# The two feed-forward products of a trunk layer by seven block products in place of eight

## The chip, the cores and the metric

The kernel runs on one core of a Trainium2 chip. The metric is the device time of one execution in microseconds (us), as a median of runs. The core has five engines that work side by side from lists of instructions of their own: TensorE (PE) for matrix products, VectorE (DVE), ScalarE (ACT), GpSimd (POOL), and SyncE (SP), which here issues nearly all transfers between DRAM and the on-chip memory. Within one list the order is fixed; between lists semaphores keep it.

## What is computed

One layer on 1024 positions of width 1024, all in float32. Three branches (an mLSTM, a differential attention, a retention) are merged and projected; then the feed-forward follows, the part that matters here:

```python
x = x + rmsnorm(y @ w_out, g[1])
h2 = rmsnorm(x, g[2])
a, u = jnp.split(h2 @ w_ffn_in, 2, axis=-1)       # [1024, 1024] @ [1024, 2 x 2816]
f = (jax.nn.silu(a) * u) @ w_ffn_out              # [1024, 2816] @ [2816, 1024]
x = x + rmsnorm(f, g[3])
```

## The kernel before

TensorE multiplies parts of 12 bits: every float32 operand is split into a high part (a cast on ScalarE, L96) and a low part (a subtraction on VectorE, L97), and `mm3` (L101 to L103) issues three matrix products of 128x128 by 128x512 for each pair of tiles. Accumulators are banks of PSUM of 128x512, four of kind "d" and four of kind "m".

All dense products of the kernel form one stream of blocks (`stream`), whose weights are loaded two blocks ahead into `ws` (two tiles), and split one block ahead into `wh` and `wl` (four tiles each). A pool "T" has 33 tiles of 4 KB for each partition and holds whatever is kept long; blocks that are marked `own` have their weights there. A pool "s2k" has eleven tiles of 128x512.

The last stage before the feed-forward is `out_blocks`. Its last quarter, `run_last`, makes the second half of the sequence tile by tile; `norm_steps` (L876 to L884) then turn each tile of the product `z` into x2 and the normalized h2, with a load of x, a square on ScalarE (L220), three single-column steps (L214, L215 on GpSimd) and wide operations on VectorE (L879, L880, L884). `transposed` (L235 to L238) turns four tiles of h2 at a time on TensorE, and splits them into `h2T`.

The hidden width of 2816 is 22 blocks of 128. For each of them `proj_half` multiplies the block's 128 columns of gate weights and of up weights (stationary, from wh/wl) with h2T (moving, 512 positions): 8 contraction tiles, 2 halves of the sequence, 3 passes each. `gated` applies Silu on ScalarE (L964), `hidden` multiplies on VectorE (L959) and splits the result into `ah`, `al`, which stay on the chip. `up_first` runs block 0 with the first half of the sequence while the second half is still being normalized. Down runs by groups of hidden blocks (2, then five times 4): for each of 8 tiles of the sequence and 2 halves of the columns it accumulates the group in PSUM and adds that into `f` (L992, L994). The last group, `last_down`, has its own weights in the big pool, and takes each finished tile through the last norm (L1016 to L1024, squares at L1037) while the next is multiplied.

SyncE issues loads and stores in the order of its list, each of them waiting for the one eight places before it.

## Time and profile before

| | us |
|---|---|
| median of three runs | 2748.53 |
| lowest and highest run | 2746.95, 2749.08 |
| span of the profiled execution | 2744.7 |
| TensorE busy in the span | 2711.7 |
| VectorE busy | 1217.4 |
| ScalarE busy | 964.1 |
| GpSimd busy | 99.2 |

The profile is of one execution on the chip. Its span runs from the first to the last recorded instruction; the time of a run holds a little more than that. An engine is busy while it executes an instruction; the matrix products of TensorE overlap, so their sum of durations is more than their busy time, and their pace is read from the distances of their starts. The chain of waits follows the work that ended last backwards. The feed-forward takes the span from about 1992 us to the end.

### The profile page before, as it was taken

To read this page: it belongs to the slowest core of one execution; us is meant where nothing else is said; L and a number is where in the kernel's file an instruction comes from. 1 tells how busy PE (TensorE), PEld (TensorE's weight loads), DVE (VectorE), ACT (ScalarE), POOL (GpSimd) and SP (SyncE) were. 2 spreads that over 40 slices of the span, in tenths; PEclk is the share of its full clock that TensorE was granted. 3 is DMA by queue.
4 is the path that set the end of the run, shared out by engine and by line. 5 is a ranking of instruction groups with operands and counts; after the bars stand their busy time and mean duration, and the time that the engine had idled before them with its cause. 6 is when DMAs were issued, how large, how long until landed. Compare 5 with 4: busy or idle time off the path is not lost.

```text
span 2744.7 us, 34888 instructions
## 1 busy us (share of the span) xinstructions
PE 2711.7 (99%) x14049; PEld 2280.3 (83%) x14049; DVE 1217.4 (44%) x2679; ACT 964.1 (35%) x1901; POOL 99.2 (4%) x165
## 2 busy tenths in 40 slices
PE   7999999999999999999999999999999999999998
PEld 6888989888888888888989888888888888888886
DVE  5565564544554545543333354354642223232315
ACT  5644443334444444444333354232521111111112
POOL 0000000000000000000000000000100000000000
PEclk9999999999999999999999999999999999999999
DMA  4121112322222213211111155422521111111113
GB/s 143 50 59 54 58 59 58 92 77 67 74 77 62 77 51 85 58 43 51 47 54 47 54 161 167 145 88 82 191 65 47 39 54 39 54 44 55 47 40 138
DMA packets 225052, 202.67 MB, mean 74 GB/s; under 512 B 9373, under 2 KB 181870, under 8 KB 224890
## 3 DMA queue, kind: packets, MB, share of 16 engines
q1 hardware_dynamic: 223456, 198.25, 23.7%
q10 hardware_dynamic: 1434, 2.20, 0.3%
q8 instruction: 110, 1.80, 0.3%
q14 instruction: 52, 0.43, 0.0%
HBM read 158.44 MB, written 33.59 MB: 70 GB/s over the span
## 4 chain that ended last, share of the span: by engine, by line
PE 94%; DVE 3%; ACT 2%; DMA 1%; issue 1%; POOL 0%; ACTq 0%; SPq 0%; POOLq 0%; DVEq 0%
PE ps L101 28%; PE ps L102 28%; PE ps L103 28%; PE ps L630 2%; PE ps L667 2%; PE ps L656 1%; PE ps L460 1%; PE ps L468 1%; DVE wl L97 0%; PE ps L428 0%; ACT wh L96 0%; PE ps L235 0%; DMA s2k<-branch 0%; PE ps L685 0%; DVE f L994 0%
## 5 line engine op out<-in xcount | busy, mean ns | idle before, releaser
L101 PE MATMUL ps<-hh,wh 128*128 128x512 f32 x1408 | 571.0, 406 | 1.6 <-DVE hl L238 1.6
L103 PE MATMUL ps<-hh,wl 128*128 128x512 f32 x1408 | 556.5, 395 | 0.0
L102 PE MATMUL ps<-hl,wh 128*128 128x512 f32 x1408 | 556.5, 395 | 0.0
L96 ACT CAST wh<-ws 128x1024 fp32r<-128x1024 f32 x219 | 228.7, 1047 | 730.0 <-PE ps L102 472.6
L97 DVE TENSOR_TENSOR wl<-ws,wh 128x1024 fp32r<-128x1024 f32 (+1 forms) x219 | 266.3, 1219 | 449.8 <-ACT wh L96 433.7
L103 PEld LDWEIGHTS ps<-hh,wl 128*128 128x128 f32 x1408 | 264.3, 188 | 63.3
L101 PEld LDWEIGHTS ps<-hh,wh 128*128 128x128 f32 x1408 | 265.1, 188 | 55.5 <-DVE hl L238 1.9
L102 PEld LDWEIGHTS ps<-hl,wh 128*128 128x128 f32 x1408 | 264.9, 188 | 53.7
L102 PE MATMUL ps<-h2l,wh 128*128 128x512 f32 x704 | 278.3, 395 | 0.0
L101 PE MATMUL ps<-h2h,wh 128*128 128x512 f32 x704 | 277.9, 395 | 0.3 <-ACT h2h L237 0.3
L103 PE MATMUL ps<-h2h,wl 128*128 128x512 f32 x704 | 278.0, 395 | 0.0
L101 PE MATMUL ps<-wh,hh 128*128 128x256 f32 (+1 forms) x768 | 219.8, 286 | 0.0
L102 PE MATMUL ps<-wl,hh 128*128 128x256 f32 (+1 forms) x768 | 216.1, 281 | 0.0
L103 PE MATMUL ps<-wh,hl 128*128 128x256 f32 (+1 forms) x768 | 215.8, 281 | 0.0
L101 PEld LDWEIGHTS ps<-h2h,wh 128*128 128x128 f32 x704 | 131.9, 187 | 32.7 <-ACT h2h L237 0.6
L102 PEld LDWEIGHTS ps<-h2l,wh 128*128 128x128 f32 x704 | 132.0, 187 | 32.2
L103 PEld LDWEIGHTS ps<-h2h,wl 128*128 128x128 f32 x704 | 132.0, 187 | 32.2
L101 PE MATMUL ps<-bh,wh 128*128 128x512 f32 x384 | 153.0, 398 | 1.0 <-ACT bh L96 1.0
L102 PE MATMUL ps<-bl,wh 128*128 128x512 f32 x384 | 151.8, 395 | 0.2 <-DVE bl L97 0.2
L103 PE MATMUL ps<-bh,wl 128*128 128x512 f32 x384 | 151.5, 395 | 0.0
L101 PEld LDWEIGHTS ps<-wh,hh 128*128 128x128 f32 x768 | 144.8, 189 | 0.2
L102 PEld LDWEIGHTS ps<-wl,hh 128*128 128x128 f32 x768 | 144.8, 189 | 0.2
(215 smaller groups left out, 4160.9 us busy)
## 6 DMA issues: line engine op xcount, KB each, us to landing
ws<-in_w_in_dram SPq DMA_DIRECT2D x110, 512.0 KB, 4.0
ws<-in_w_ffn_in_dram SPq DMA_DIRECT2D x44, 512.0 KB, 4.0
gate<-s2k SPq DMA_DIRECT2D x48, 256.0 KB, 2.0
gl<-gate SPq DMA_DIRECT2D x24, 512.0 KB, 6.2
s2k<-branch SPq DMA_DIRECT2D x48, 256.0 KB, 5.6
ws<-in_w_ffn_out_dram SPq DMA_DIRECT2D x22, 512.0 KB, 4.3
dk<-dk SPq DMA_DIRECT2D x64, 128.0 KB, 2.3
ws<-in_w_out_dram SPq DMA_DIRECT2D x16, 512.0 KB, 3.9
```

The costliest lines, as they stand in the source:

```text
L96: nc.scalar.copy(hi, src)
L97: nc.vector.tensor_sub(lo, src, hi.bitcast(F32))
L101: nc.tensor.matmul(ps, lh, rh, start=start, stop=False)
L102: nc.tensor.matmul(ps, lh, rl, start=False, stop=False)
L103: nc.tensor.matmul(ps, ll, rh, start=False, stop=stop)
L460: nc.tensor.matmul(ps[:, :P], k_t[c // 4][:, j, half_cols(c)], q_t[c // 4][:, j, half_cols(c)], start=j == 0, stop=j == 1)
L468: nc.tensor.transpose(ps[:, j * P:(j + 1) * P], hn[:, j * P:(j + 1) * P], ident)
L630: nc.tensor.matmul(ps[:, :b - a], d["q", qb // 4][:, c, half_cols(qb)], d["k", n][i][:, c, :b - a], start=i == 0, stop=i == 1)
L656: nc.tensor.transpose(ps[:, i * P:(i + 1) * P], u["sb"][0][:, kb * P:(kb + 1) * P], ident)
L667: nc.tensor.matmul(o_ps[:, :P], u["at"][kb // 4][:, half_cols(kb)], v[kb // 4][:, kb % 4, vc], start=kb == 0, stop=kb == qb)
```

## The change

Up and down are each written as a product of 2 x 2 blocks, and each by Strassen's method in Winograd's form: seven block products of sums of blocks in place of eight block products. For up, the left operand h2 is cut by halves of the sequence and halves of the contraction (A11 to A22), the right by halves of the contraction and by gate and up columns (B11 to B22), one hidden block at a time. For down, it is halves of the sequence by even and odd hidden blocks on the left, even and odd hidden blocks by halves of the columns on the right.

`turned` takes the place of `transposed`: it keeps the unsplit transposed tile too (`hx`), and `left_sums` makes the sums S1 to S4 of it and splits them. `Up.sums` makes the sums of the weights (T1 to T4) on VectorE. The seven products of a block share two banks of PSUM: a bank is read after a product and further products are then added into it. Blocks 0 and 1 run interleaved; from block 2 on the order is p1, p2, p6, p5, p7, p3, p4. The hidden values are not split; `keep_hidden` stores for each pair of blocks three of them and four sums, which GpSimd makes, into tables `hid` in DRAM: seven tiles of 256 KB a pair. All of up is done before down. `down` runs seven products after another; each goes through all 11 pairs, and for each pair it reads one tile of `hid`, splits it, makes the weights' sum in place, splits that (both into wh/wl), and multiplies four tiles of the sequence: 12 matrix products. All row blocks of `w_ffn_out` are loaded once and stay.

The core of the diff, with blank lines left out; `Block`, `stream` and the other stages are as before:

```diff
-    h2T = Act("h2")
-        turns = {sh: transposed(h2T, z[sh], sh, 80) for sh in range(2)}
+        turns = {sh: turned(z[sh], sh, 80) for sh in range(2)}
...
         def run_last(w):
             before = []
+            ups[0].load()
...
             z[0][:] = [None] * 4
+            ups[0].split("B1")
...
-    def hidden(blk, sh, pu):
...
-    def gated(blk, sh, pa):
...
-    def up_first(blk, turns):
...
-    def down(blks, st, ch, w, first):
...
-    def last_down(blks):
...
+    NP = FB // 2
+    ROLES = ("A11", "A12", "A22", "S1", "S2", "S3", "S4")
+    hid = {r: dram.tile([NP, P, HALF], F32, name=f"hid_{r}") for r in ROLES}
...
+    def turned(src, sh, g):
+        for kt in range(KT) if sh == 0 else (4, 5, 0, 1, 6, 7, 2, 3):
+            ps = psum()
+            for i in range(4):
+                nc.tensor.transpose(ps[:, i * P:(i + 1) * P], src[i][:, kt * P:(kt + 1) * P], ident)
+            col = pcol[:, g + kt:g + kt + 1]
+            role, q = "A" + str(sh + 1) + str(kt // 4 + 1), kt % 4
+            if (role, q // 2) not in h2x:
+                h2x[role, q // 2] = big([P, 2, HALF], name="hx")
+            x = h2x[role, q // 2][:, q % 2, :]
+            if role == "A21":
+                nc.scalar.activation(x, ps, AF.Copy, scale=col)
+            else:
+                h, l = h2.slot(role, q)
+                nc.scalar.activation(h, ps, AF.Copy, scale=col)
+                nc.vector.tensor_scalar(x, ps, col, None, op0=ALU.mult)
+                nc.vector.tensor_sub(l, x, h.bitcast(F32))
+            yield
+    def left_sums():
+        for i in range(2):
+            nc.vector.tensor_add(h2x["A22", i], h2x["A21", i], h2x["A22", i])
+            h2.put("S1", i, h2x["A22", i])
+        yield
+        for i in range(2):
+            nc.vector.tensor_sub(h2x["A22", i], h2x["A22", i], h2x["A11", i])
+            h2.put("S2", i, h2x["A22", i])
...
+    class Up:
+        def __init__(self, blk, own=False):
+            self.blk, self.own, self.w = blk, own, {}
+        def load(self):
+            self.raw = [pool.tile([P, KT, P], F32, tag="ws", bufs=N_WS, name=nm("ws")) if not self.own else big([P, KT, P], name="ws")
+                        for _ in range(2)]
+            for u in range(2):
+                nc.sync.dma_start(self.raw[u], cols_of(w_ffn_in, u * FF + self.blk * P)[0])
+        def sums(self):
+            a, u = self.raw
+            self.t13 = big([P, KT, P], name="t13")
+            self.t24 = big([P, KT, P], name="t24")
+            lo, hi = slice(0, 4), slice(4, 8)
+            nc.vector.tensor_sub(self.t13[:, lo, :], u[:, lo, :], a[:, lo, :])
+            nc.vector.tensor_sub(self.t13[:, hi, :], u[:, hi, :], u[:, lo, :])
+            nc.vector.tensor_add(self.t24[:, lo, :], self.t13[:, hi, :], a[:, lo, :])
+            nc.vector.tensor_sub(self.t24[:, hi, :], a[:, hi, :], self.t24[:, lo, :])
...
+        def product(self, ps, right, left, more):
+            wh, wl = self.w.pop(right)
+            for q in range(4):
+                mm3(ps, (wh[:, q, :], wl[:, q, :]), h2.slot(left, q), q == 0 and not more, q == 3, more)
+        def p1(self):
+            self.x = psum(True)
+            self.product(self.x, "B11", "A11", False)
+            self.a = half_tile()
+            nc.scalar.copy(self.a, self.x)
+        def p2(self):
+            z = psum(True)
+            self.product(z, "B21", "A12", False)
+            nc.vector.tensor_add(self.a, z, self.a)
+            nc.scalar.activation(self.a, self.a, AF.Silu)
...
+        def p7(self):
+            self.product(self.x, "T3", "S3", True)
+            nc.vector.tensor_add(self.e, self.x, self.e)
+        def p3(self):
+            self.product(self.y, "B22", "S4", True)
+            nc.vector.tensor_add(self.b, self.y, self.b)
+            nc.vector.tensor_mul(self.b, self.a, self.b)
+            self.h = [self.b, self.e]
+        def p4(self):
+            self.product(self.x, "T4", "A22", True)
+            s = half_tile()
+            nc.scalar.activation(s, self.x, AF.Silu)
+            nc.vector.tensor_mul(self.e, s, self.e)
+            self.x = self.y = self.a = self.b = self.e = None
+    def keep(role, p, t):
+        nc.sync.dma_start(hid[role][p], t)
+    def keep_hidden(first, second):
+        p = first.blk // 2
+        (a11, a21), (a12, a22) = first.h, second.h
+        keep("A11", p, a11)
+        keep("A12", p, a12)
+        keep("A22", p, a22)
+        s = [half_tile() for _ in range(4)]
+        nc.gpsimd.tensor_tensor(s[0], a21, a22, op=ALU.add)
+        keep("S1", p, s[0])
+        nc.gpsimd.tensor_tensor(s[2], a11, a21, op=ALU.subtract)
+        keep("S3", p, s[2])
+        nc.gpsimd.tensor_tensor(s[1], s[0], a11, op=ALU.subtract)
+        keep("S2", p, s[1])
+        nc.gpsimd.tensor_tensor(s[3], a12, s[1], op=ALU.subtract)
+        keep("S4", p, s[3])
+        first.h = second.h = None
+    def feed_forward(ups, turns):
+        a, b = ups[:2]
+        a.sums()
+        for what in ("T24", "T13", "B2"):
+            a.split(what)
+        a.p1()
+        a.p2()
+        b.load()
+        b.sums()
+        b.split("B1")
+        b.p1()
+        for _ in turns:
+            pass
+        z[1][:] = [None] * 4
+        sums = left_sums()
+        next(sums)
+        b.p2()
+        for what in ("T24", "T13", "B2"):
+            b.split(what)
+        a.p5(False)
+        next(sums)
+        b.p5(False)
+        a.p6()
+        next(sums)
+        b.p6()
+        a.p7()
+        next(sums)
+        b.p7()
...
+        keep_hidden(a, b)
+        for n, u in enumerate(ups[2:], 2):
+            after = ups[n + 1] if n + 1 < len(ups) else None
+            u.p1()
+            if after is not None:
+                after.load()
+            u.p2()
+            u.p6()
+            if after is not None:
+                after.sums()
+            u.p5()
+            if after is not None:
+                after.split("B1")
+            u.p7()
+            if after is not None:
+                after.split("T24")
+            u.p3()
+            if after is not None:
+                after.split("T13")
+            u.p4()
+            if after is not None:
+                after.split("B2")
+            if n % 2:
+                keep_hidden(ups[n - 1], u)
+        for r in ROLES:
+            h2.drop(r)
+    def down():
+        gains[3] = gain(3)
+        f = [None] * NT
+        w = []
+        def load(p):
+            w.append([big([P, D], name="wd") for _ in range(2)])
+            for i in range(2):
+                nc.sync.dma_start(w[p][i], w_ffn_out[(2 * p + i) * P:(2 * p + i + 1) * P, :])
+        def right(role, p):
+            b11, b12, b21, b22 = (w[p][i][:, halfs(ch)] for i in range(2) for ch in range(2))
+            if role == "B11":
+                return b11
+            if role == "T1":
+                nc.vector.tensor_sub(b12, b12, b11)
+                return b12
...
+            nc.vector.tensor_sub(b12, b21, b12)
+            return b12
+        def operands(role_l, role_r, p):
+            t = half_tile()
+            nc.sync.dma_start(t, hid[role_l][p])
+            h = pool.tile([P, 2, HALF], F32R, tag="wh", bufs=N_WH, name=nm("wh"))
+            l = pool.tile([P, 2, HALF], F32R, tag="wl", bufs=N_WL, name=nm("wl"))
+            split_sbuf(h[:, 0, :], l[:, 0, :], t)
+            split_sbuf(h[:, 1, :], l[:, 1, :], right(role_r, p))
+            return h, l
+        def step(ps, o, j, first, last, more):
+            h, l = o
+            c = slice(j * P, (j + 1) * P)
+            mm3(ps, (h[:, 0, c], l[:, 0, c]), (h[:, 1, :], l[:, 1, :]), first and not more, last, more)
+        def product(role_l, role_r, ps, more):
+            for p in range(NP):
+                if role_r == "B11":
+                    load(p)
+                o = operands(role_l, role_r, p)
+                for j in range(4):
+                    step(ps[j], o, j, p == 0, p == NP - 1, more)
...
+        f[:] = [big([P, D], name="f") for _ in range(NT)]
+        px = [psum(True) for _ in range(4)]
+        product("A11", "B11", px, False)
+        for j in range(4):
+            nc.scalar.copy(f[j][:, halfs(0)], px[j])
+        py = [psum() for _ in range(4)]
+        product("S1", "T1", py, False)
...
+        product("S4", "B22", py, True)
+        for j in range(4):
+            nc.vector.tensor_add(f[j][:, halfs(1)], py[j], f[j][:, halfs(1)])
+        product("S3", "T3", px, True)
...
+        pz = [psum() for _ in range(4)]
+        product("A12", "B21", pz, False)
+        for j in range(4):
+            nc.vector.tensor_add(f[j][:, halfs(0)], pz[j], f[j][:, halfs(0)])
+        s2 = [small([P, 2], "s2", bufs=8) for _ in range(NT)]
+        held = []
+        for p in range(NP):
+            o = operands("A22", "T4", p)
+            if p < NP - 4:
+                for j in range(4):
+                    step(px[j], o, j, False, False, True)
+                if p < 4:
+                    xt = x2_of(p)
+                    for ch in range(2):
+                        squares(p, ch, s2[p])
+                    finish(p, xt, s2[p])
+                    f[p] = None
+                    squares(p + 4, 1, s2[p + 4])
+            else:
+                held.append(o)
+        xts = [x2_of(j + 4) for j in range(4)]
+        for j in range(4):
+            for n, o in enumerate(held):
+                step(px[j], o, j, False, n == 3, True)
+            st = j + 4
+            squares(st, 0, s2[st], px[j])
+            nc.vector.tensor_copy(f[st][:, halfs(0)], px[j])
+            finish(st, xts[j], s2[st])
...
-    groups = [[0, 1]] + [list(range(i, i + 4)) for i in range(2, FB, 4)]
...
-            blocks += [up_first(blk, turns)] if blk == 0 else up_blocks(blk)
...
+    ups = [Up(i, own=i == 1) for i in range(FB)]
...
     for _ in dense:
         pass
+    feed_forward(ups, turns)
+    down()
```

Three places where the lists of the engines differ. Names are those of the program with a number; "waits" lists the semaphores that a row waits for (DMAHW: a transfer's).

SyncE, where the second half of the sequence is normalized (`xr` is x, `x2_dram` takes x2, `ws` are weights). Before:

```order
L876 DMA xr_3778_18307<-in_x_dram 128x1024 [waits DMAHW1_49,DMAHW0_49]
L876 DMA xr_3792_18369<-in_x_dram 128x1024
L139 DMA ws_3862_18756<-in_w_ffn_out_dram 128x2x512 [waits DMAHW6_49,DMAHW2_49,DVE_49]
L881 DMA x2_dram_78<-xr_3778_18307 128x1024 [waits DMAHW3_49,DVE_49]
L881 DMA x2_dram_78<-xr_3792_18369 128x1024 [waits DVE_49]
```

After:

```order
L876 DMA xr_3775_18310<-in_x_dram 128x1024 [waits DMAHW3_49,Activation_49]
L881 DMA x2_dram_78<-xr_3775_18310 128x1024 [waits DMAHW6_49,DVE_49]
L876 DMA xr_3790_18375<-in_x_dram 128x1024 [waits DMAHW7_49,PE_49]
L876 DMA xr_3805_18440<-in_x_dram 128x1024 [waits DMAHW0_49,PE_49]
L876 DMA xr_3815_18486<-in_x_dram 128x1024 [waits DMAHW1_49,PE_49]
L881 DMA x2_dram_78<-xr_3790_18375 128x1024 [waits DMAHW2_49,DVE_49]
```

Before, the x of the first and of the second tile were asked for one after the other, ahead of the first store of x2; now the store of the first tile's x2 stands between them.

VectorE, same place. Before, the last two tiles' norms and what follows them (L959 is block 0, L238 the transposed tiles; `xs`, `xv` are single columns):

```order
L879 SCALAR_TENSOR_TENSOR z_3767_18253<-z_3767_18253,xr_3819_18482,gain1_3661_17745 128x1024 [waits Pool_49]
L880 TENSOR_TENSOR xr_3816_18477<-xr_3816_18477,z_3767_18253 128x1024 [waits DMAHW6_49,DVE_49]
L214 TENSOR_SCALAR xv_3824_18493<-xs_3822_18490 128x1 [waits Activation_49]
L884 TENSOR_SCALAR z_3767_18253<-xr_3816_18477,xr_3823_18492 128x1024 [waits Pool_49]
L959 TENSOR_TENSOR s2k_3829_18528<-ps_3830_18530,s2k_3829_18528 128x512 [waits PE_49,Activation_49]
L97 TENSOR_TENSOR al_3832_18556<-s2k_3829_18528,ah_3831_18555 128x512 [waits Activation_49]
L238 SCALAR_TENSOR_TENSOR h2l_3835_18566<-ps_3833_18560,pcol_83,h2h_3834_18565 128x512 [waits Activation_49]
L238 SCALAR_TENSOR_TENSOR h2l_3835_18566<-ps_3836_18569,pcol_83,h2h_3834_18565 128x512 [waits Activation_49]
```

After, from the second tile's sum of x and z on (t13, t24 are weight sums, L97 with `wl` a split of weights):

```order
L880 TENSOR_TENSOR xr_3790_18375<-xr_3790_18375,z_3764_18255 128x1024 [waits DMAHW7_49]
L1043 TENSOR_TENSOR t13_3826_18510<-ws_3768_18262,ws_3767_18261 128x512 [waits DMAHW4_49,PE_49]
L1044 TENSOR_TENSOR t13_3826_18510<-ws_3768_18262 128x512
L215 TENSOR_SCALAR xv_3803_18415<-xs_3801_18412 128x1 [waits Activation_49]
L1045 TENSOR_TENSOR t24_3827_18511<-t13_3826_18510,ws_3767_18261 128x512 [waits DVE_49,PE_49]
L884 TENSOR_SCALAR z_3764_18255<-xr_3790_18375,xr_3802_18414 128x1024 [waits Pool_49]
L1046 TENSOR_TENSOR t24_3827_18511<-ws_3767_18261,t24_3827_18511 128x512 [waits DVE_49]
L215 TENSOR_SCALAR xv_3809_18446<-xs_3807_18443 128x1 [waits Activation_49]
L879 SCALAR_TENSOR_TENSOR z_3765_18257<-z_3765_18257,xr_3808_18445,gain1_3661_17752 128x1024 [waits Pool_49]
L97 TENSOR_TENSOR wl_3829_18517<-t24_3827_18511,wh_3828_18516 128x1024 [waits Activation_49]
L880 TENSOR_TENSOR xr_3805_18440<-xr_3805_18440,z_3765_18257 128x1024 [waits DMAHW0_49,DVE_49]
```

Before, the norms stood nearly alone; now weight sums and splits of blocks 0 and 1 stand between the steps of the norms.

SyncE at the end of up. Before, the weights of the last blocks and of the last group of down:

```order
L139 DMA ws_4263_22192<-in_w_ffn_in_dram 128x8x128 [waits DMAHW5_49,DVE_49]
L139 DMA ws_4270_22252<-in_w_ffn_in_dram 128x8x128 [waits DMAHW6_49,DVE_49]
L139 DMA ws_4277_22316<-in_w_ffn_out_dram 128x2x512 [waits PE_49]
L139 DMA ws_4278_22318<-in_w_ffn_out_dram 128x2x512 [waits PE_49]
L139 DMA ws_4279_22320<-in_w_ffn_out_dram 128x2x512 [waits PE_49]
```

After, the last stores of hidden values and sums, and the first reads of down:

```order
L1109 DMA hid_A22_88<-s2k_4310_21506 128x512 [waits DMAHW0_49,DVE_49]
L1109 DMA hid_S1_89<-s2k_4312_21553 128x512 [waits DMAHW1_49,Pool_49]
L1109 DMA hid_S3_91<-s2k_4314_21555 128x512 [waits DMAHW2_49,Pool_49]
L1109 DMA hid_S2_90<-s2k_4313_21554 128x512 [waits DMAHW3_49,Pool_49]
L1109 DMA hid_S4_92<-s2k_4315_21556 128x512 [waits DMAHW4_49,Pool_49]
L1229 DMA s2k_4331_21583<-hid_A11_86 128x512 [waits DMAHW5_49,Activation_49]
L1229 DMA s2k_4336_21607<-hid_A11_86 128x512 [waits DMAHW6_49,Activation_49]
```

The reads of `hid_A11` come in the list behind the stores of the last pair, which wait for GpSimd; before, only weights were moved there.

## Rows read from the trace of the kernel before

**Rows 1.** The page: busy time by engine; the chain of waits by engine.
```profile
PE 2711.7 (99%) x14049; PEld 2280.3 (83%) x14049; DVE 1217.4 (44%) x2679; ACT 964.1 (35%) x1901; POOL 99.2 (4%) x165
...
PE 94%; DVE 3%; ACT 2%; DMA 1%; issue 1%; POOL 0%; ACTq 0%; SPq 0%; POOLq 0%; DVEq 0%
```

**Rows 2.** Windows in the feed-forward: length, busy by engine, granted clock, DMA share, GB/s.
```profile
2064.00:2155.00 91.00, 91.00 (x392) 73.10 (x391) 21.11 (x25) 18.04 (x25) 0.00 (x0) 1.00 0.15 47
2155.00:2694.00 539.00, 539.00 (x2313) 433.38 (x2311) 145.65 (x179) 86.66 (x112) 0.00 (x0) 1.00 0.16 50
```

**Rows 3.** Groups by line, up (page: busy, mean ns, idle) and down (durations).
```profile
L101 PE MATMUL ps<-h2h,wh 128*128 128x512 f32 x704 | 277.9, 395 | 0.3 <-ACT h2h L237 0.3
...
L101 PE MATMUL ps<-wh,ah x352: 389/395/397, 2041.0 to 2733.4; 128*128 128x512 f32 x176
```

**Rows 4.** Timeline of TensorE: start, duration, instruction; up, then the last group of down.
```profile
2012.07 0.40 PE L103 MATMUL ps<-h2h,wl 128*128 128x512 f32 x1
...
2016.27 0.40 PE L101 MATMUL ps<-h2h,wh 128*128 128x512 f32 x1
...
2727.32 0.39 PE L101 MATMUL ps<-wh,ah 128*128 128x512 f32 x1
...
2733.66 0.39 PE L102 MATMUL ps<-wl,ah 128*128 128x512 f32 x1
2733.89 0.39 PE L103 MATMUL ps<-wh,al 128*128 128x512 f32 x1
```

**Rows 5.** Groups of VectorE and ScalarE from 1940 on: busy, mean ns, idle before.
```profile
L97 DVE TENSOR_TENSOR wl<-ws,wh 128x1024 fp32r<-128x1024 f32 x71 | 86.5, 1223 | 217.4 <-ACT wh L96 205.4 <-PE ps L102 11.8
...
L97 DVE TENSOR_TENSOR al<-s2k,ah 128x512 fp32r<-128x512 f32 x44 | 30.3, 688 | 15.8 <-ACT ah L96 15.8
L1022 DVE SCALAR_TENSOR_TENSOR f<-f,xr,gain 128x512 f32<-128x512 f32 x16 | 11.3, 748 | 5.8 <-POOL xr L215 5.8
...
L879 DVE SCALAR_TENSOR_TENSOR z<-z,xr,gain 128x1024 f32<-128x1024 f32 x8 | 10.2, 1282 | 3.3 <-POOL xr L215 3.3
...
L884 DVE TENSOR_SCALAR z<-xr,xr 128x1024 f32<-128x1024 f32 x8 | 6.0, 753 | 2.7 <-POOL xr L215 2.6
...
L96 ACT CAST wh<-ws 128x1024 fp32r<-128x1024 f32 x69 | 72.5, 1051 | 368.9 <-PE ps L102 176.1 <-PE ps L103 103.6 <-issue 78.6
L96 ACT CAST ah<-s2k 128x512 fp32r<-128x512 f32 x44 | 27.2, 618 | 111.6 <-DVE s2k L959 111.6
L964 ACT ACTIVATE s2k<-ps 128x512 f32<-128x512 f32 x44 | 26.2, 595 | 99.7 <-PE ps L103 99.6
```

**Rows 6.** Groups of GpSimd, whole span: busy, mean ns, idle before.
```profile
L215 POOL TENSOR_TENSOR dfac<-dv,expo 128x1 f32<-128x1 f32 x64 | 35.2, 550 | 661.0 <-DVE dv L214 661.0
L215 POOL TENSOR_TENSOR xr<-xv,expo 128x1 f32<-128x1 f32 x32 | 25.5, 801 | 1044.3 <-DVE xv L214 1044.3
```

**Rows 7.** Timeline of TensorE: last product of out, first of up, first transposes of the second half.
```profile
1991.85 0.40 PE L103 MATMUL ps<-wh,yl 128*128 128x512 f32 x1
1992.09 0.39 PE L101 MATMUL ps<-h2h,wh 128*128 128x512 f32 x1
...
2003.28 0.93 PE L235 MATMUL ps<-ident,z 128*128 128x128 f32 x7
```

**Rows 8.** DMA issues, whole span: count, KB each, median us from issue to landing.
```profile
ws<-in_w_ffn_in_dram SPq DMA_DIRECT2D x44, 512.0 KB, 4.0
gate<-s2k SPq DMA_DIRECT2D x48, 256.0 KB, 2.0
...
xr<-in_x_dram SPq DMA_DIRECT2D x8, 512.0 KB, 5.5
...
x<-x_dram SPq DMA_DIRECT2D x8, 512.0 KB, 9.2
```

**Rows 9.** Windows at the end of the span, columns as in rows 2.
```profile
2694.00:2700.00 6.00, 6.00 (x28) 4.99 (x27) 2.36 (x6) 1.45 (x4) 0.55 (x1) 1.00 1.02 414
...
2734.00:2739.00 5.00, 0.28 (x2) 0.00 (x0) 3.45 (x8) 1.45 (x4) 0.52 (x1) 1.00 0.28 105
...
2740.00:2744.00 4.00, 0.00 (x0) 0.00 (x0) 1.68 (x3) 0.00 (x0) 0.00 (x0) 0.50 0.35 131
```

165 lines of the change are left out of this document (87 added, 78 removed).

## The prediction

> **What bounds the kernel now.** I read the busy shares and the chain of waits first: TensorE is busy for 2711.7 of 2744.7 us and carries 94% of the chain [rows 1]. The windows over the feed-forward say the same more sharply: from 2064 to 2155 (up) and from 2155 to 2694 (up and down by turns) TensorE has no idle time at all, VectorE is busy for 146 and ScalarE for 87 of 539 us, and the DMA engines run at a share of 0.16 [rows 2]. So a matrix product that goes away is worth its whole interval there, until something else becomes late. The interval is read from starts in the timeline, not from the durations (0.39 to 0.40 us, which overlap): 18 intervals from 2012.07 to 2016.27 give 0.2333 us, and 28 from 2727.32 to 2733.66 give 0.2265 us [rows 4]. The slower rate stands where one operand lies in the small pool wh/wl, the faster in the last group, whose weights lie in the big one.
>
> **What goes.** Up has 704 products of each of three passes, down 352 [rows 3]: 2112 + 1056 = 3168. Afterwards up has 22 blocks x 7 x 4 x 3 = 1848, down 7 x 11 x 4 x 3 = 924: 2772. TensorE's list of instructions is shorter by 397 rows, so the change does what it says. Before: 2976 x 0.2333 + 192 x 0.2265 = 737.8 us. After, all operands of down in wh/wl: 2772 x 0.2333 = 646.7. **Gain 91.1 us.** The unknown is the rate of down's new products: both operands now come from wh/wl, which no row shows. At 0.2265 it is 6.2 us more gain, as much the other way at 0.240 (the same step upward); I take 0.2333, the rate with one operand there.
>
> **Steady up stage.** A block is 7 x 12 x 0.2333 = 19.6 us of TensorE. VectorE has in it 4 sums and one split of 512, 3 splits of 1024, 5 evacuations of 512: 10 x 0.69 + 3 x 1.22 = 10.6 us; ScalarE 3 x 1.05 + 0.62 + 5 x 0.60 = 6.8 us [rows 5]. Both fit. GpSimd gets four sums of 128x512 for each pair of blocks; its only rows are 128x1 at 0.55 to 0.80 us [rows 6]. I price the wide one as that start-up plus VectorE's 0.69 for the same width, 1.24 us; the bounds are 0.69 (no dearer than VectorE) and 1.93 (0.55 + two times 0.69). At 5 us in 39 us nobody waits for it. The Trainium skill, GPSIMD Engine Reference, 3.1 Elementwise, has a sum of 2048 elements at 4497 ns on GpSimd and 2293 on VectorE; by that ratio, an estimate, the wide sum takes 1.35 us, and the time below grows by 0.4. Seven stores of 256 KB and four weight loads of 512 KB per pair are 3.8 MB in 39.2 us, some 97 GB/s, against 414 GB/s where the trace is saturated [rows 9]. The tightest chain is the second weight half of the next block: its buffer is free 1.5 us into the block, it lands after 4.0 us [rows 8], two sums, the evacuations behind them in VectorE's order and a copy follow, and product seven at 11.2 us needs that; I find 2.1 us of slack. Cost 0, bounds 0 and 0.5 us x 20 = 10 us.
>
> **Front (start of the feed-forward).** Before, TensorE ended `out` at 1992.1 and had 48 products of block 0 to run until the transposes of the second half at 2003.28 [rows 7]: the norms were covered. Now A22, A21 and the sums S1 and S2 must exist before the two first blocks go beyond p1 and p2, and VectorE makes most of it in order. In its order, the sum of x and z of the second tile of that half (first row of the second VectorE piece, L880) waits for an x load that is now issued behind the store of the tile before it; with 5.5 us to land [rows 8] I put it at 1990.5. From there to the split of S2 there are 18 operations of 1024 at 1.22, two at 1.28, three at 0.75 and 20 of 512 at 0.69 [rows 5], and five tiny ones: 22.0 + 2.6 + 2.3 + 13.8 + 0.7 = 41.4 us. That ends at 2032 with no waits; with 4 us of waits for ScalarE's casts and squares between (bounds 0 and 4, and 0.04 to 0.07 us less per operation where such are back to back), between 2029 and 2036. From there 90 products remain of both blocks, 21.0 us: 2050 to 2057. With TensorE never waiting, the 168 products and 32 transposes (0.93 us for seven [rows 7], so 4.3 us) from 1991.5 would end at 2035.0. **Stall 15 to 22 us, taken 18**; bounds 10 (a third of VectorE's work slipped under waits that I count) and 24.
>
> **Junction from up to down.** On SP's list the first read of `hid_A11` stands behind the store of the last `hid_S4`, and that one waits for GpSimd, though A11 was stored long before. From the end of the last product: Silu 0.60, multiply 0.69, four sums on GpSimd 4 x 1.24 = 5.0, semaphores and issue 0.6 (an estimate, no row has them apart), landing 2.5 (between 2.0 for 256 KB and 4.0 for 512 KB [rows 8], nearer the first), cast 0.62, split 0.69 [rows 5]: **10.7 us** in which TensorE has nothing. With GpSimd at 0.69 or 1.93 it is 8.5 or 13.5, with a landing of 5.5 us 13.7; with both late 17. The sums of GpSimd run beside VectorE's sums for T1 and its splits. The Trainium skill, SBUF — State Buffer, Who interferes with whom, says that a VectorE instruction with two inputs in SBUF and a GpSimd instruction that reads SBUF exclude each other; that speaks against this part, and by it each of the four could wait one 0.69 us operation more, 2.8 us in all, and the time would be 2696 in place of the 2693 below. No row here shows the two together, so the sum goes without it; the bounds hold it.
>
> **The clock.** The granted clock is 1.00 to 2739, 5 us after the last product, and 0.50 from 2740 on [rows 9]: 2.4 GHz falls to 1.2 after that much idleness. A gap of 10.7 us is longer, so down starts at half speed. No row shows how it comes back; I take one step of 12 products at 5.6 instead of 2.8 us, **2.8 us**, bounds 0 and 5.6. The same happens in the front, but there TensorE runs behind VectorE anyway.
>
> **Steady down, and its end.** A step is 12 products, 2.8 us; it needs two casts of 512 (1.24 us of ScalarE) and two splits and one sum (2.07 us of VectorE), and a read of 256 KB, 94 GB/s. Reads run ahead by the 11 buffers of s2k, splits by 4 of wh/wl, and the two sets of PSUM banks change places, so evacuations are hidden: cost 0. In the last product VectorE has 11 x 2.07 + four finishes of two L1022 and two adds, 4 x 2.9 [rows 5], + 4 x 0.69 = 37.1 us against 30.8 of TensorE; a lead of some 3 to 6 us covers part: **3.6 us**, bounds 0 and 8. After the last product 10.4 us came before (it ends at 2733.89 + 0.39 [rows 4]); the same chain of square, norm, scale, add and store remains: +0.3, bounds -1 and +4.
>
> **Sum.** 2744.7 - 91.1 + 18 + 10.7 + 2.8 + 3.6 + 0.3 = 2689.0 us of span. The three runs have a median of 2748.5, 3.8 above the span: 2693. All lows together (10, 8.5, 0, 0, -1, rate -6.2) give 2669; all highs (24, 17, 5.6, 8, 4, blocks 10, rate 6.2) 2732.
>
> **Rivals.** *Only the products count.* Front and junction are hidden, as the front is before [rows 7]: 2744.7 - 91.1 + 3.8 = 2657. For it: TensorE bound everywhere in [rows 2]. Against it: nothing stands in TensorE's list to fill the junction, and VectorE's work in the front is longer than the products beside it. 6%.
> *Down runs one step after another.* If cast, sum and splits do not run ahead, a step takes 2 x 0.62 + 3 x 0.69 = 3.3 us instead of 2.8 [rows 5], 77 x 0.5 = 39 us: 2732. For it: every operand of every product is now loaded and split anew, where before a split weight tile served eight row tiles. Against it: four buffers, and both engines have time over. 10%.
> *Slower: each up block waits for its weights.* The second half of the next block's weights is asked for only when a split frees its buffer, and SP's list puts it among stores that wait for GpSimd. With the landing at 9.2 us, which loads of 512 KB took in the last stretch [rows 8], instead of 4.0, the slack of 2.1 is overrun by 3.1 us, x 20 blocks = 62 us: 2755, slower than before. It decides from a landing of 8.9 us (55 us / 20 = 2.8 over the slack). Against it: 9.2 us belong to a stretch with a DMA share near 1 [rows 9], and the up stage needs a quarter of that. 11%.
> *No difference*: a mixture of the two last, 3%.
>
> **Chances.** The forecast, with its bounds of 2669 to 2732, has 70%; with the clean cut and the serial down that makes 86% faster. A measurement of this kernel tells about 0.2%, 5.5 us, from no change: same 3%, slower 11%. The range runs from 2668 to 2733, which takes in the serial down and leaves out the clean cut, the slower case and no change, 20%.
>
> **What would show it.** In the changed kernel's profile: intervals of 0.233 us in up and down, a block each 19.6 us and a step each 2.8 us; TensorE idle for some 15 to 20 us in all between 1995 and 2035 with VectorE full there; one gap of 9 to 14 us at the junction with the granted clock at 0.5 behind it; VectorE near full in the last 30 us. The forecast is wrong if up blocks take over 20 us, if down steps take over 3 us, or if the front's idle time is under 10 or over 24 us.

## The result and the profile after

The changed kernel takes 2687.46 us (median of 4 runs, 2687.34 to 2689.41) against 2747.88 for the kernel before in the same comparison: a ratio of 0.9783, 95% interval 0.9769 to 0.9797, 60 us faster. The forecast was 2693, with a range of 2668 to 2733.

The page of the profile after, first the busy time by engine, then the chain of waits by engine (compare [rows 1]):

```profile
span 2685.7 us, 35232 instructions
...
PE 2624.1 (98%) x13653; PEld 2212.7 (82%) x13653; DVE 1403.5 (52%) x2953; ACT 1089.1 (41%) x2119; POOL 161.7 (6%) x209
...
PE 78%; issue 14%; DVE 3%; DMA 2%; POOL 1%; ACT 1%; SPq 0%; ACTq 0%; DVEq 0%; POOLq 0%
```

TensorE has 396 products less and is busy for 98% of the span; the 14% of issue in the chain are hardly idle time of TensorE, since it is idle for only 61.6 us in the whole span (2685.7 - 2624.1). What it waits for from 1940 us on is a short list; the columns are what waited, for whom, us in total, times, and the longest:

```profile
PE ps L102 <- ACT wh L96: 15.1, 2, 10.7
PE ps L990 <- DVE xv L215: 4.3, 1, 4.3
PE ps L103 <- DVE S1l L97: 3.6, 1, 3.6
PE ps L102 <- ACT S1h L96: 1.8, 1, 1.8
PE ps L103 <- DVE xv L215: 1.1, 1, 1.1
```

The single wait of 10.7 us is the junction; the other 4.4 us of that line, and the lines of L990, S1l and S1h, are the front; the last line is in the last of down's seven products. The windows (length, busy by engine, granted clock, DMA share, GB/s, as [rows 2]) show the stages: the front, steady up, the junction, the start of down, steady down, the end.

```profile
1992.27:2036.80 44.53, 29.16 (x115) 21.95 (x114) 37.09 (x48) 26.63 (x39) 4.23 (x5) 0.81 0.28 94
2200.00:2400.00 200.00, 200.00 (x859) 160.82 (x858) 108.81 (x135) 67.95 (x93) 26.96 (x20) 1.00 0.30 99
2446.00:2460.00 14.00, 3.35 (x14) 2.46 (x13) 3.74 (x6) 1.71 (x3) 5.34 (x4) 0.68 0.70 247
2460.00:2490.00 30.00, 30.00 (x124) 24.51 (x124) 20.07 (x32) 13.55 (x26) 0.00 (x0) 0.92 0.78 290
2500.00:2640.00 140.00, 140.00 (x619) 115.98 (x618) 86.28 (x134) 63.20 (x112) 0.00 (x0) 1.00 0.40 124
2640.00:2676.00 36.00, 32.29 (x140) 25.73 (x138) 31.49 (x61) 19.39 (x49) 4.81 (x6) 1.00 0.20 74
```

Steady up and steady down have no idle TensorE at all. The pace, from the timeline of TensorE (start, duration): up from 2104.35 to 2107.15 is 12 intervals of 0.2333, as before; down from 2560.22 to 2564.07 is 17 intervals of 0.2265.

```profile
2104.35 0.39 PE L102 MATMUL ps<-S1h,wh 128*128 128x512 f32 x1
...
2107.15 0.39 PE L102 MATMUL ps<-S3h,wh 128*128 128x512 f32 x1
...
2560.22 0.39 PE L103 MATMUL ps<-wl,wh 128*128 128x512 f32 x1
...
2564.07 0.39 PE L102 MATMUL ps<-wh 128*128 128x512 f32 x1
```

With that each term of the sum can be measured in the span. A term's "after" is worked out from starts on TensorE: run_last ends and block 0 begins at 1992.27, the last product of up starts at 2448.52 (and takes one interval, to 2448.75), the first of down starts at 2459.56, the last of down at 2673.66.

| term | forecast | after | how |
|---|---|---|---|
| products | -91.1 | -97.0 | 1848 x 0.2334 + 924 x 0.2267 against 737.8 |
| front | +18 | +20.9 | 1992.27 to 2448.75 is 456.5; less 431.3 of products and 4.3 of transposes |
| junction | +10.7 | +10.8 | 2448.75 to 2459.56 |
| half clock behind it | +2.8 | +2.4 | 11 intervals to 2464.42 take 4.86 in place of 2.49 |
| last of down's seven products | +3.6 | +2.5 | 2459.56 to 2673.66, less 923 x 0.2267 and the 2.4 |
| after the last matrix product | +0.3 | +1.2 | 11.65 us against 10.4 |
| sum | -55.7 | -59.2 | the span fell by 59.0 |

Block 1 has its weights and their splits in T, and its 84 products run at 0.227 and not at 0.2334; counted so, 0.6 us more go to the gain of the products and 0.6 us more to the front.

### The profile page after: what moved, and what is told of

It reads as the page before. It is cut to its first block, busy times and chain, and to the rows that moved or that the text cites. A ratio compares the mean times of both kernels' runs of the same rounds, so it can differ in the third digit from the quotient of the medians.

```text
span 2685.7 us, 35232 instructions
## 1 busy us (share of the span) xinstructions
PE 2624.1 (98%) x13653; PEld 2212.7 (82%) x13653; DVE 1403.5 (52%) x2953; ACT 1089.1 (41%) x2119; POOL 161.7 (6%) x209
## 4 chain that ended last, share of the span: by engine, by line
PE 78%; issue 14%; DVE 3%; DMA 2%; POOL 1%; ACT 1%; SPq 0%; ACTq 0%; DVEq 0%; POOLq 0%
PE ps L103 23%; PE ps L104 23%; PE ps L102 23%; PE ps L631 2%; PE ps L668 2%; PE ps L657 1%; PE ps L461 1%; DVE wl L97 1%; DMA hid_S<-s2k 1%; PE ps L469 1%; POOL xr L216 0%; PE ps L429 0%; DMA s2k<-branch 0%; PE ps L686 0%; POOL s2k L1125 0%
## 5 line engine op out<-in xcount | busy, mean ns | idle before, releaser
L96 ACT CAST wh<-ws 128x1024 fp32r<-128x1024 f32 (+1 forms) x197 | 196.1, 999 | 431.1 <-PE ps L103 366.7
L97 DVE TENSOR_TENSOR wl<-ws,wh 128x1024 fp32r<-128x1024 f32 (+2 forms) x197 | 227.6, 1158 | 243.6 <-ACT wh L96 238.9
L102 PEld LDWEIGHTS ps<-hh,wh 128*128 128x128 f32 x1408 | 265.8, 189 | 55.7 <-DVE hl L239 2.3
L104 PEld LDWEIGHTS ps<-wh,hl 128*128 128x128 f32 x768 | 144.9, 189 | 0.0
L102 PE MATMUL ps<-wh 128*128 128x512 f32 x308 | 120.4, 393 | 10.7 <-ACT wh L96 10.7
L103 PE MATMUL ps<-wl,wh 128*128 128x512 f32 x308 | 121.2, 393 | 1.8 <-DVE xv L215 1.1
L104 PE MATMUL ps<-wh,wl 128*128 128x512 f32 x308 | 120.8, 392 | 0.0
L638 ACT ACTIVATE sb<-sb,nmx 128x896 f32<-128x896 f32 (+7 forms) x128 | 98.6, 771 | 50.3 <-DVE nmx L637 49.7
L96 ACT CAST wh<-s2k 128x512 fp32r<-128x512 f32 x77 | 47.7, 620 | 113.1 <-PE ps L104 103.4
```

What stands on the lines that cost most here:

```text
L96: nc.scalar.copy(hi, src)
L97: nc.vector.tensor_sub(lo, src, hi.bitcast(F32))
L102: nc.tensor.matmul(ps, lh, rh, start=start, stop=False, skip_group_check=more)
L103: nc.tensor.matmul(ps, lh, rl, start=False, stop=False, skip_group_check=more)
L104: nc.tensor.matmul(ps, ll, rh, start=False, stop=stop, skip_group_check=more)
L638: nc.scalar.activation(sb[c], sb[c], AF.Exp, bias=nmx, scale=slope, accum_out=sm[:, c:c + 1])
```

## The experiments

Unless it says otherwise, an experiment starts from the changed kernel and makes one edit; the fifth builds on the fourth, and the eleventh joins several.

**1. One offset for both operands.** The rate of down was the term that was sized worst. The addresses of the tiles show that T begins 32 bytes behind a multiple of 64, and wh and wl on a multiple. One single-column buffer more takes 32 bytes for each partition and moves wh and wl by as much.

```diff
-        t = small([P, 1], tag + "v", bufs=4)
+        t = small([P, 1], tag + "v", bufs=5 if tag == "x" else 4)
```

> One edit on the changed kernel: one more single-column buffer (32 bytes for each partition) ahead of the pools wh and wl. The big pool T begins 32 bytes behind a multiple of 64, wh and wl on a multiple; with the edit all three begin 32 bytes behind. Theory (the interval of two 128x512 products depends on whether stationary and moving operand start at the same offset within 64 bytes: it was 0.2267 us where both lie in T and, after the change, where both lie in wh/wl, and 0.2333 where one lies in each): up's interval falls from 0.2333 to 0.2267, down's stays at 0.2267; 7452 products of 512 columns in the whole kernel change, 7452 x 0.0067 = 50 us, so about 2638 us, less if the narrower ones gain too. Rival (the rate goes with the stage or with the pool and not with the address): intervals stay as they are, within 2 us of 2687.

2655.64 us (2653.75 to 2656.5), ratio to the kernel before 0.9663 (0.9648 to 0.9677): 32 us faster than the changed kernel, less than 50. Up's intervals did fall: in the timeline of TensorE 19 from 2103.97 to 2108.28 are 0.2268. The narrower products did not follow: 23 intervals of 256 columns, at the same place of the stage of the branches' projections, take 2.76 us here and took 2.72 in the changed kernel (the last two pairs of lines; the first of them is the changed kernel).

```profile
2103.97 0.39 PE L102 MATMUL ps<-S3h,wh 128*128 128x512 f32 x1
...
2108.28 0.39 PE L103 MATMUL ps<-S4l,wh 128*128 128x512 f32 x1
...
216.00 0.28 PE L102 MATMUL ps<-wh,hh 128*128 128x256 f32 x1
...
218.72 0.28 PE L104 MATMUL ps<-wh,hl 128*128 128x256 f32 x1
...
213.56 0.28 PE L102 MATMUL ps<-wh,hh 128*128 128x256 f32 x1
...
216.32 0.28 PE L104 MATMUL ps<-wh,hl 128*128 128x256 f32 x1
```

From the first product with A22 to the last it is 385.5 us in place of 396.9, and 1704 x 0.0067 = 11.4 is the whole of that. The merge stage (1152 products) got 6.0 of its 7.7 us. The projections of the branches, with 4224 products of 512, gave only 13 of 28 us. By the starts on TensorE the products of 512 gained 18.6 us, running among others as they do there; the 2112 products of 256, whose operands agree now too, lost 2.9 us, and the remaining 2.7 us went to transposes and to the changes from one kind to another. So the rate of products of 512 goes with the placement, the narrower ones go slightly the other way, and the estimate for the rest of the kernel was too high.

**2. The same in the kernel before.** The same line.

> The kernel before with the same 32 bytes ahead of wh and wl as in the first experiment. Theory: its feed-forward has 2976 products of 512 columns with one operand in T and one in wh/wl, the changed kernel 1848; 1128 x 0.0067 = 7.5 us more gain than the 32 us there, so about 2708 us; with both placed alike the seven products then give 53 us in place of 60. Rival (the placement helps only the changed kernel): within 20 us of 2747.

2707.04 us (2704.74 to 2707.39), ratio 0.9852 (0.9835 to 0.9868): as the theory says. In windows of the same length TensorE starts 1964 products in place of 1909 (the first line is the kernel before):

```profile
2155.00:2600.00 445.00, 445.00 (x1909) 357.81 (x1908) 121.88 (x151) 66.95 (x87) 0.00 (x0) 1.00 0.16 47
...
2155.00:2600.00 445.00, 445.00 (x1964) 368.45 (x1964) 121.74 (x148) 73.26 (x95) 0.00 (x0) 1.00 0.18 52
```

With both kernels placed alike the change gives 2707.0 - 2655.6 = 51.4 us. The other 9 of its 60 us are the products fewer that run at the slower rate: 1128 by the expectation, 1212 when block 1's 84 are left out of the changed kernel's (8.1 us by the count), most of them because down's operands happened to move into pools of one offset.

**3. Half of it.** 32 bytes between wh and wl.

```diff
                         hi = pool.tile(shape, F32R, tag="wh", bufs=N_WH, name=nm("wh"))
+                        if not pad:
+                            pad.append(small([P, 8], "pad", bufs=1))
+                            nc.vector.memset(pad[0], 0.0)
```

> The changed kernel with 32 bytes put between the pools wh and wl: wl then starts at the same offset within 64 bytes as T, wh still 32 bytes off. In up the pass with the low weights (wl stationary, T moving) agrees, the two with wh do not; in down the pass high by high agrees (both in wh), the two with one operand in wl do not. Theory (offset of stationary against moving operand within 64 bytes): one interval of three is 0.2267 and two are 0.2333 in up and in down, a mean of 0.231 in both; down gets slower by 616 x 0.0067 = 4 us, up faster by as much; time near 2680 (other stages gain a third of what the first experiment gave). Rival (only the distance of T from wh counts, or something else that the first edit moved): up stays at 0.2333 or down at 0.2267 throughout.

One run, 2693.52 us: a miss. In windows of the same length up has the same 636 products in 148 us as before the edit, and down 605 in place of 619 in 140 us.

```profile
2052.00:2200.00 148.00, 148.00 (x636) 119.11 (x635) 80.99 (x100) 50.41 (x69) 22.11 (x16) 1.00 0.34 109
2500.00:2640.00 140.00, 140.00 (x605) 113.20 (x604) 86.05 (x133) 61.79 (x110) 0.00 (x0) 1.00 0.40 126
```

Down did get slower once its two pools disagreed, as the placement explains, but one agreeing pass of three bought up nothing, and down pays 0.232 in place of the 0.231 that a sum by passes gives. The trace shows where up's gain went: from 2052 to 2448 the start behind the agreeing pass comes after 0.231 us in the mean, but the one behind the next pass after 0.236, so the two cancel. With two passes of three disagreeing nearly the whole price is paid. Why a pass's neighbour pays stays open, and one run of this kernel tells little of its whole time.

**4. Reads ahead of the last stores.**

```diff
+        if second.blk == FB - 1 and not late:
+            late.append((first, second))
+            return
         s = [half_tile() for _ in range(4)]
...
                 o = operands(role_l, role_r, p)
+                if role_r == "B11" and p == 3:
+                    keep_hidden(*late[0])
```

> One edit on the changed kernel: the last pair's four sums on GpSimd and their stores are put behind the first four reads of down, nothing else. Theory (the 10.8 us at the junction are the chain of GpSimd sums and stores in front of the first read on SyncE's list, and the half clock behind it comes from that gap): the gap goes below 2 us, the first products run at 0.2267, the time falls by 9 to 13 us, to about 2676. Rival (the first step waits for the weights of down, which take 7.3 us to land at a DMA share near 0.7): the gap stays above 6 us and the time falls by less than 4 us.

2680.68 us (2678.93 to 2683.52), ratio 0.9755 (0.9739 to 0.9771): 6.8 us faster, between the two. The gap fell from 10.7 to 3.3 us, and was not gone because the first read still stood behind the store of A12, which waits for a multiply of the last block. What came in its place is in the timeline of VectorE and GpSimd at the junction:

```profile
2453.29 1.68 DVE L97 TENSOR_TENSOR wl<-s2k,wh 128x512 fp32r<-128x512 f32 x1 [1.24 <-ACT wh L96]
...
2454.38 1.73 POOL L1129 TENSOR_TENSOR s2k<-s2k,s2k 128x512 f32<-128x512 f32 x1
...
2454.89 1.76 DVE L97 TENSOR_TENSOR wl<-wd,wh 128x512 fp32r<-128x512 f32 x1
```

VectorE's splits, 0.69 us elsewhere, take 1.7 beside GpSimd's sums, and three of the four sums take 1.6 to 1.7 instead of 1.3. This is the rule of the Trainium skill that the prediction weighed (SBUF — State Buffer, Who interferes with whom): the two exclude each other. Its price for a split of 512 is 1.0 us here. In the changed kernel itself VectorE had one weight sum beside the first of GpSimd's sums and nothing to split, so it cost some 0.4 us there (1.64 in place of 1.25), not 2.8.

**5. Three reads still earlier**, in the last block of up, added to the fourth edit.

```diff
             u.p7()
+            if after is None:
+                for p in range(3):
+                    early.append(half_tile())
+                    nc.sync.dma_start(early[p], hid["A11"][p])
```

> As the second experiment (the last pair's sums on GpSimd and their stores behind the first reads of down), and the first three reads are issued already in the last block of up. There the gap was 3.3 us and the time fell by 6.8, because the first read still stood behind a store of the last pair. Theory: the first step's operands are split before the last product ends, the gap goes to below 1 us; the time falls by 9 to 12 us against the changed kernel, to 2676 to 2679. VectorE's splits beside GpSimd's four sums take 1.7 us in place of 0.69 as there, so TensorE waits again for some 1 to 2 us. Rival (the weights' landing, or the splits beside GpSimd, take the place of the gap): as in the second experiment, 2680 or more.

2676.24 us (2675.75 to 2677.12), ratio 0.9741 (0.9727 to 0.9756), 11.2 us faster. Up's last product and down's first are one stream now, 0.23 us apart, and nothing of the half clock is left (granted 1.00 from 2449 to 2470); TensorE's one wait in down up to 2640 is of 1.2 us, twelve us later.

```profile
2448.73 0.40 PE L104 MATMUL ps<-A22h,wl 128*128 128x512 f32 x1
2448.97 0.39 PE L102 MATMUL ps<-wh 128*128 128x512 f32 x1
...
2461.24 0.50 PE L102 MATMUL ps<-wh 128*128 128x512 f32 x1 [1.21 <-ACT wh L96]
```

So the junction was the order of SyncE's list with GpSimd's chain in it, not the landing of the weights.

**6. Down with eight products.**

```diff
-        product("S2", "T2", px, True)
...
+        product("A11", "B11", px, False)
+        product("A12", "B21", px, True)
...
+        product("A11", "B12", py, False)
+        product("A12", "B22", py, True)
...
```

> Half of the change undone: up as in the changed kernel, down by eight block products with the same reads, splits and steps; the four sums of GpSimd and the sums of the down weights are gone, four tables of hidden values are stored in place of seven. Theory: 132 more products of 0.2267 = 29.9 us; the junction loses the GpSimd chain of 5.5 us, and up to 2.4 us of half clock with it; the last product has less VectorE work, up to 2 us: 2707 to 2712. So down's part of the gain is 20 to 24 us net and up's the rest. Rival (the reads and splits of down were hidden only just, or the junction is the weights' landing): 2715 or more.

2710.16 us (2709.93 to 2710.59), ratio 0.9865 (0.9851 to 0.988). The seven products in place of eight give 22.7 us net in down. The rest, 36 us, is up's part together with what down's new placement gives: the 864 products of down that ran at 0.2333 before run at 0.2267 in both of these kernels, 5.7 us by the count. The gap at the junction is 5.4 us here, without GpSimd.

**7 to 9. The front.** Three edits that take VectorE's work in the front apart. Block 1's weight sums and first product later:

```diff
         b.load()
-        b.sums()
-        b.split("B1")
-        b.p1()
         for _ in turns:
             pass
...
         next(sums)
+        b.sums()
+        b.split("B1")
+        b.p1()
         b.p2()
```

> One edit on the changed kernel: the weight sums, the split and the first product of block 1 stand behind the transposes of the second half and behind S1, in place of ahead of them. Theory (the 21 us of stall in the front are VectorE's work in order, plus 4.2 us in which VectorE itself waited because the transposes stood behind block 1's first product at half clock): S1 and S2 are ready 5 to 9 us earlier, the stall falls by 3 to 8 us, to about 2682. Rival (VectorE's total work up to S4 sets the end, whatever its order): within 2 us of 2687.

2689.36 us (2688.45 to 2693.18), ratio 0.9789 (0.9774 to 0.9804): no gain. S1 was ready 4.6 us earlier (its last split ends at 2023.2 in place of 2027.8; the run is 0.9 us ahead there from the second tile on), but block 1's sums then stood in front of S2, whose last split ended at 2037.0 in place of 2036.3.

The weight sums of blocks 0 and 1 on GpSimd:

```diff
+            eng = nc.gpsimd if self.blk < 2 else nc.vector
-            nc.vector.tensor_sub(self.t13[:, lo, :], u[:, lo, :], a[:, lo, :])
+            eng.tensor_tensor(self.t13[:, lo, :], u[:, lo, :], a[:, lo, :], op=ALU.subtract)
...
```

> One edit on the changed kernel: the eight weight sums of 512 columns of blocks 0 and 1 go from VectorE to GpSimd. Theory (VectorE's work in order sets the front's stall): 8 x 0.69 = 5.5 us less of it, the stall falls by 3 to 5 us, to about 2683. First rival (a VectorE operation with two inputs in the on-chip memory and a GpSimd operation exclude each other): VectorE's operations beside the sums get longer by about as much, no gain, within 1.5 us of 2687. Second rival (the sums, 1.3 us each, stand in GpSimd's order ahead of the norms' single-column steps): each norm of the second half is later, 2 to 6 us slower.

2689.83 us (2688.92 to 2692.48), ratio 0.979 (0.9775 to 0.9804): no gain, 2.4 us slower by medians. Both rivals are in its timeline of VectorE:

```profile
1990.09 2.75 DVE L1002 TENSOR_TENSOR A12l<-hx,A12h 128x512 fp32r<-128x512 f32 x2
1992.75 2.32 DVE L880 TENSOR_TENSOR xr<-xr,z 128x1024 f32<-128x1024 f32 x1
...
2008.07 1.75 DVE L884 TENSOR_SCALAR z<-xr,xr 128x1024 f32<-128x1024 f32 x1 [2.35 <-POOL xr L216]
```

Two operations of L1002 take 2.75 where they took 1.28, a sum of 1024 takes 2.32 in place of 1.22, and the norm waits 2.35 us for a single-column step that stood behind the sums in GpSimd's list.

The same sums left out, so that the products of blocks 0 and 1 use unsummed weights:

```diff
             a, u = self.raw
+            if self.blk < 2:
+                self.t13, self.t24 = u, a
+                return
```

> The changed kernel, with the eight weight sums of blocks 0 and 1 left out (their products use unsummed weights). Theory (VectorE's work in order sets the front's stall of 21 us): 5.5 us less of it, the stall falls by 3 to 5.5 us, to 2682 to 2684. Rival (the stall is set by the chain of the last tile's norm, the transposes and S1, and by what TensorE has left to do after that, and VectorE only fills the gaps): within 1.5 us of 2687.

2679.14 us (2678.68 to 2682.28), ratio 0.9755 (0.974 to 0.9769): 8.3 us faster, more than the 5.5 of work that went. S2's last split ended at 2029.5 (the second line; the first is the changed kernel).

```profile
2035.07 1.23 DVE L97 TENSOR_TENSOR S2l<-hx,S2h 128x1024 fp32r<-128x1024 f32 x1 [0.85 <-ACT S2h L96]
...
2028.28 1.22 DVE L97 TENSOR_TENSOR S2l<-hx,S2h 128x1024 fp32r<-128x1024 f32 x1
```

VectorE's own wait of 4.2 us for the transposes fell to 0.5 as well, which would make up the rest. So the stall follows the amount of VectorE's work ahead of S2; the one other order that was tried bought nothing.

**10. S1 out of the accumulator.**

```diff
+                if role == "A22":
+                    nc.vector.scalar_tensor_tensor(x, ps, col, h2x["A21", q // 2][:, q % 2, :], op0=ALU.mult, op1=ALU.add)
+                    nc.vector.scalar_tensor_tensor(l, ps, col, h.bitcast(F32), op0=ALU.mult, op1=ALU.subtract)
...
-            nc.vector.tensor_add(h2x["A22", i], h2x["A21", i], h2x["A22", i])
```

The A21 tiles are also transposed ahead of the A22 tiles, since the sum needs them.

> One edit on the changed kernel: S1 is formed as the transposed tile leaves the accumulator (one operation that scales and adds A21, one that scales and subtracts the high part), in place of a scaled copy, a subtraction and a sum; the A21 tiles are transposed ahead of the A22 tiles. VectorE's work up to S2 falls by 2 x 1.22 us, and one sum for S3 moves behind S2. Theory (VectorE's work in order sets the front's stall): 2 to 4 us faster, 2683 to 2686. Rival (the transposes stand behind block 1's first product, and that sets it): within 1.5 us of 2687.

2684.81 us (2684.23 to 2690.07), ratio 0.9776 (0.9762 to 0.9791): 2.7 us faster by medians, which its interval does not separate from none. In the profiled execution the way from block 0's first product to the first with A22 is 57.9 in place of 58.9 us. It has the sign of the theory; the size is not settled.

**11. Together**: the offset, the early reads with the last pair's sums on VectorE, and S1 out of the accumulator.

```diff
         s = [half_tile() for _ in range(4)]
+        eng = nc.vector if second.blk == FB - 1 else nc.gpsimd
```

> The changed kernel with the 32 bytes of the first experiment, the early reads of the ninth, the last pair's four sums on VectorE in place of GpSimd, and the sums of the tenth. Theory (the three gains lie in different places and add up): 2655.6 - 9 to 12 - 2 to 4 = 2640 to 2645, and no VectorE operation of over 0.8 us at the junction. Rival (the junction's or the front's gain comes back later, in the last product, where VectorE is near full): 2648 or more.

2639.3 us (2638.03 to 2641.24), ratio 0.9606 (0.959 to 0.9622): the gains add up (31.8, 11.2 and 2.7 by themselves, 48.2 together; the sums on VectorE are new in it). This kernel is 48 us faster than the changed one, and 108 us faster than the one before. At the junction the clock stays at 1.00 and TensorE does not pause; the splits are back at 0.69 us. The columns of the second part are busy us and mean ns in the groups of VectorE from 2410 to 2425:

```profile
2412.00:2416.00 4.00, 4.00 (x19) 3.34 (x18) 3.77 (x8) 2.26 (x4) 0.00 (x0) 1.00 0.85 329
2416.00:2420.00 4.00, 4.00 (x20) 3.30 (x19) 3.96 (x8) 1.14 (x2) 0.00 (x0) 1.00 0.76 266
...
L97 DVE TENSOR_TENSOR wl<-s2k,wh 128x512 fp32r<-128x512 f32 x6 | 4.1, 685 | 2.7 <-ACT wh L96 2.7
```

## Why the prediction was right, and where not

The forecast's case came true: a gain of whole products, less a stall in the front, a gap at the junction and a slow restart. By its steps:

**The products** were right in number. The rate was the step that was mis-sized: it took 0.2333 for down "with one operand" in wh/wl, and down runs at 0.2267, the lower of its bounds, 6.1 us better. Both rates were there [rows 4], and the pools were named; what was not asked is why two operands in T should be faster than one. Experiments 1 and 2 put it down to placement; the third leaves open how the price falls on the single pass.

**The front** was sized well (18 forecast, 20.9 measured) and its steps hold: the second tile's sum of x and z started at 1990.46 (forecast 1990.5), S2's last split ended at 2036.3 (forecast 2029 to 2036). But one reason was wrong: that sum did not wait for x; VectorE had been busy without a pause up to it, so that the start agrees is luck. From there to the end of S2 two errors offset: VectorE was busy for 38.4 us, where 41.4 of work were counted, and idle for 7.4, where 0 to 4 were allowed.

```profile
1987.94 1.40 DVE L1001 TENSOR_SCALAR hx<-ps,pcol 128x512 f32<-128x512 f32 x2
1989.26 1.28 DVE L1002 TENSOR_TENSOR A12l<-hx,A12h 128x512 fp32r<-128x512 f32 x2
1990.46 1.22 DVE L880 TENSOR_TENSOR xr<-xr,z 128x1024 f32<-128x1024 f32 x1
```

Another was incomplete. The prediction had TensorE's clock fall in the front at no cost, since TensorE ran behind VectorE. In the front TensorE is idle for 15.4 us (the first window above); the other 5.5 us of the 20.9 are mostly products at half speed. One stretch of them stood in VectorE's way: block 1's first product waited for its weights and ran at 0.43 us an interval, granted clock 0.50, with the transposes behind it, and VectorE waited 4.2 us for those. That wait is more than half of VectorE's idle time above; the forecast had put its 4 us down to ScalarE's casts and squares. What the half speed by itself costs in the end is not shown: experiment 7 took that product out of the way and gained nothing.

```profile
2008.28 0.80 PE L102 MATMUL ps<-A11h,wh 128*128 128x512 f32 x1 [4.41 <-ACT wh L96]
...
2012.31 0.63 PE L104 MATMUL ps<-A11h,wl 128*128 128x512 f32 x1
2012.74 0.63 PE L102 MATMUL ps<-A11h,wh 128*128 128x512 f32 x1
...
2014.76 0.60 PE L990 MATMUL ps<-ident,z 128*128 128x128 f32 x4
...
2016.17 1.41 DVE L1001 TENSOR_SCALAR hx<-ps,pcol 128x512 f32<-128x512 f32 x2 [4.16 <-ACT A22h L1000]
```

**The junction** was right, 10.8 against 10.7, and link by link: GpSimd's four sums take 1.64, 1.25, 1.26 and 1.26 us (1.24 forecast), the first read is issued at 2456.20 behind the last store, and its cast starts 2.7 us later (2.5). The estimate from the Trainium skill (GPSIMD Engine Reference, 3.1 Elementwise) was 1.35 us for a sum, 0.1 above the three that ran alone.

```profile
2450.34 1.64 POOL L1119 TENSOR_TENSOR s2k<-s2k,s2k 128x512 f32<-128x512 f32 x1 [33.30 <-DVE s2k L1105]
...
2454.50 1.26 POOL L1125 TENSOR_TENSOR s2k<-s2k,s2k 128x512 f32<-128x512 f32 x1
2456.20 3.72 SPq L1229 DMA_DIRECT2D s2k<-hid_A  x8
2458.89 0.62 ACT L96 CAST wh<-s2k 128x512 fp32r<-128x512 f32 x1 [9.35 <-DMA s2k<-hid_A]
...
2459.56 0.79 PE L102 MATMUL ps<-wh 128*128 128x512 f32 x1 [10.65 <-ACT wh L96]
```

**The clock** restarted at half speed (granted 0.50 from 2459.6 to 2464.4), for about the one step that was assumed. **Steady up and down** cost nothing, as forecast: up's weights land in 3.9 us, a down step in 12 x 0.2267. **The end** was near: 2.5 and 1.2 in place of 3.6 and 0.3.

**The rivals.** The clean cut (2657) fell with the front and the junction, 31.7 us together. Down step after step fell: no idle time on TensorE in the window from 2500 to 2640. The up block that waits for its weights fell: 200.00 us busy of 200.

Two errors offset in part: the rate (6.1 better) against the front (2.9 worse); the rest is under 1.5 us each. The span itself came out 3.3 us below the forecast's 2689.0. What lies outside the span was 1.8 us here where 3.8 was taken: the 3.8 is the median of all runs less the span of one profiled execution.

## What to carry to other kernels

An algorithm with fewer products pays in the steady state by the full interval of each product, and loses at the seams: price each seam by walking every engine's list, above all the queue of transfers, in which a read of data that lies ready can stand behind a store that waits. Take elementwise work off the path by removing it: putting it into another order, or giving it to GpSimd beside a busy VectorE, bought nothing here. Where one kind of instruction has two rates in a trace, find out what separates them before pricing a change that moves its operands.

## What the runs showed of the hardware that was not expected

Products of 128x512 follow each other at 0.2267 us when stationary and moving operand both start on a multiple of 64 bytes (down in the changed kernel) or both 32 bytes behind one (the last group before, up in experiment 1), and at 0.2333 when one does this and the other that, whichever of the two is the stationary one. 32 bytes of padding were worth 32 us in the changed kernel and 40 in the one before. With one pass of three agreeing, up stayed at 0.2333 and down came to 0.232. Products of 256 columns are the exception: 0.1183 us an interval with the operands 32 bytes apart, 0.1200 with both alike, in the stretch shown in experiment 1. Other distances than 0 and 32 bytes were not tried, and what in the chip makes this, and the price per pass, were not settled.
